# Five edits to the seams of a PE-bound fp32r network kernel: mixer output, rotation tables, lag-kernel join, re-layouts, input buffers

## The chip, the core and the metric

One program on one core of a Trainium2 chip. The metric is the device time of one execution in microseconds; the kernel before ran in 1490.31, 1491.07 and 1494.53 us, median 1491.07 us.

## The reference, cut to what matters

Two blocks of two layers on a 256 x 1024 activation, all in float32. Every norm is an rms norm over the row.

```
x += rms(even_mixer(rms(x)));   x += rms(cross_attn(rms(x), mem));  x += rms(mlp(rms(x)))    # layer 0
x += rms(band_attn(rms(x)));    x += rms(cross_attn(rms(x), mem));  x += rms(mlp(rms(x)))    # layer 1
x += diff_attn(rms(x));         x += mlp(rms(x))                                             # second block
x += s5(rms(x));                x += mlp(rms(x))

even_mixer(h): u, q, f, i, g = split(h @ w_in)
    o = gated_recurrence(q, k(f), i, log f)                 # 4 heads of 128
    return concat(pooled(u), rmsnorm(o) * out_gain * silu(g)) @ w_out
diff_attn(u):  q, k, v = split(u @ w_qkv)                   # 8 heads, two maps each
    q, k = rope(rms(q) * q_gain), rope(rms(k) * k_gain)     # cos and sin tables
    a = softmax(q0 k0) - lam * softmax(q1 k1)               # lam from four vectors
    return rms(a @ v) * subln * (1 - lam_init) @ w_o
s5(u): y = scan(u; A, B, C) + reversed scan(u; ...) + d * u # 64 groups of 16 channels, 64 states
    val, gate = split(gelu(y) @ w_glu);  return val * sigmoid(gate)
mlp(h): return relu(h @ w1)**2 @ w2                         # 1024 -> 4096 -> 1024
```

## The kernel before, in words

X lies in SBUF as two token tiles t of 128 rows by 1024. Each weight is loaded by SP in 512 KB pieces (`raw`, L42) and split into a high part `whi` (ACT, L47 or L53 with a gain) and a low part `wlo` (DVE, L49 or L58, some on POOL). Each product takes three matmuls on PE (L217 to L219 for 128x512, L224 to L226 for 128x256). X reaches the feature layout through PE transposes (`tp`, L140), a copy `hh` on ACT (L143) and a difference `hl` on DVE (L144).

`mlp` (L275) has eight chunks: chunks 0 and 1 through `ff1_a` and transposes (`fftp`, L345), the rest through `ff1_b`, each followed by the `ff2` of the chunk two before it into the accumulators `ffacc`; the last `ff2` takes two chunks and ends token tile 0 ahead of tile 1, each with `done`, that is `residual` (L178): mean square `ms` on ACT (L168), `r` on DVE and POOL (L170, L171), X on DVE (L200). Between its steps an MLP draws pieces from a generator `fill`. In the MLP of layer 1 that is `ssm_tables` for blocks 0 to 7, in the first MLP of the second block the same for blocks 8 to 15, then `ssm_prefetch`.

Per block, `ssm_tables` loads `bc`, `pk` and `gb` (SP), forms `bb`, `er` and `gr` by complex products (`cmul`: DVE, with the products `cmt` of some on POOL, L1165 and L1166), writes `gr` to DRAM (`d_g`), transposes `er` on PE (`etp`) and writes it (`d_e`), forms the lag kernels `kl` and writes them (`d_kl`, L1434). After its eight blocks it joins them in DRAM (`d_ks`, two DMAs, L1450 and L1451) and spreads them to step tables (`d_tt`, eight DMAs, L1456), all issued by POOL.

In the middle of the layer-1 MLP `reorder` writes X to DRAM and loads it back in another token order (L1791); `scales` then takes the row scale of the reordered X again, from inside chunk 5 (L383 to L389). `diff` (L639) loads its cosines, sines, gains and lambda vectors at its start, turns them into the rotation tables `ta` and `tb` (L656 to L674), then projects k, q and v; `prep` normalises and rotates a projected part (`y` on POOL L731, `z` on DVE) before it is transposed (`tq`). `ssm` (L1497) lays X out by groups (`xp`: 48 copies over DVE, ACT and POOL, L1522 to L1526), transposes (`utp`), and forms states and outputs from units `e`, `g` and `t` that SP loads from `d_e`, `d_g` and `d_tt` (L1482). In the even mixer, `vg` (L1092) takes each token tile's recurrence `o`, normalises it into `y` (L1119 to L1124) and transposes it (`otp`, L1127); `proj_a` then accumulates `pacc`.

The order on each engine is set by a planner that walks the program in the written order with priorities: `low(n)` lets instructions be taken n steps later, `now()` and `turns` say how far a projection goes before it takes up the callbacks that wait in `later`, and `manual_schedule(engines=...)` keeps the written order on the named engines. Pools whose tiles wait by tile decide when a buffer is free.

## Time and profile before

| | |
|---|---|
| profiled execution | 1488.93 us, of which span 1487.2 us |
| median of three runs | 1491.07 us |
| PE busy | 1414.7 us, 95% |
| DVE, ACT, POOL busy | 74%, 58%, 16% |
| chain that ended last | PE 73%, DVE 13%, DMA 6%, issue 4%, ACT 3% |
| mean granted TensorE clock | 0.985 of full speed |

Stages along the span, in us: even mixer 0 to 140, cross attention to 270, MLP to 470, band and cross attention to 640, MLP of layer 1 to 847, diff attention to 965, MLP to 1183, s5 to 1285, last MLP to the end. PE is the engine to look at first; what it does not do is a list of gaps, each with what ended it, and stretches at a clock of 0.50.

### The profile page before, as it was taken

Reading aid. Unit: us, or ns where it says so; the run is one execution under the profiler, and the core shown is the slowest. Engines: PE = TensorE matmul, PEld = TensorE weight load, DVE = VectorE, ACT = ScalarE, POOL = GpSimd, SP = SyncE. Lnnn points to the kernel's source line nnn. Section 1 sums busy time; section 2 is a strip of 40 time slices with the busy share of each in tenths; the row PEclk is TensorE's granted clock in tenths of the full one; section 3 lists DMA queues with packets and bytes.
Section 4 is the critical chain, followed back from the end, with each engine's and each line's share of the span. In section 5 each row is a group of like instructions: output and inputs, shape, how many; then the busy total and the mean of one; then the engine's idle time right before and its main releaser. Section 6 shows DMA issues by size and latency. Waiting matters only on the chain.

```text
span 1487.2 us, 25549 instructions
## 1 busy us (share of the span) xinstructions
PE 1414.7 (95%) x9668; PEld 1231.5 (83%) x9668; DVE 1103.8 (74%) x1965; ACT 859.4 (58%) x1480; POOL 234.4 (16%) x290
## 2 busy tenths in 40 slices
PE   8899999999999999999999789999999878999997
PEld 8897888998889798878888667888889666889895
DVE  7996658997676866569998589889995487665651
ACT  7475547565564665566656557667656463554540
POOL 1232001000010000014634210033551200000000
PEclk9999999999999999999999999999999998999999
DMA  8465535475875356366677734357779977455640
GB/s 302 143 198 170 185 125 177 157 257 193 287 256 184 119 180 200 112 207 207 220 242 265 254 124 142 100 161 241 238 236 334 346 280 262 153 187 180 210 159 29
DMA packets 121236, 298.26 MB, mean 201 GB/s; under 512 B 15129, under 2 KB 24121, under 8 KB 120473
## 3 DMA queue, kind: packets, MB, share of 16 engines
q1 hardware_dynamic: 113848, 271.40, 55.3%
q0 software_dynamic: 7264, 25.24, 4.6%
q8 instruction: 76, 1.25, 0.3%
q14 instruction: 48, 0.39, 0.1%
HBM read 270.15 MB, written 31.62 MB: 203 GB/s over the span
## 4 chain that ended last, share of the span: by engine, by line
PE 73%; DVE 13%; DMA 6%; issue 4%; ACT 3%; POOL 1%; SPq 0%; DVEq 0%; ACTq 0%; POOLq 0%
PE ffacc L217 7%; PE ffacc L219 7%; PE ffacc L218 7%; PE ffps L224 5%; PE ffps L226 5%; PE ffps L225 5%; PE pacc L219 4%; PE pacc L218 4%; PE pacc L217 4%; DVE wlo L58 3%; PE pb L225 3%; PE pb L224 3%; PE pb L226 3%; DMA raw<-in_w_ff 2%; PE ffps L219 2%
## 5 line engine op out<-in xcount | busy, mean ns | idle before, releaser
L58 DVE SCALAR_TENSOR_TENSOR wlo<-raw,gcols,whi 128x512 fp32r<-128x512 f32 (+1 forms) x456 | 356.7, 826 | 75.6 <-ACT whi L53 75.3
L53 ACT ACTIVATE whi<-raw,gcols 128x512 fp32r<-128x512 f32 (+1 forms) x456 | 317.0, 745 | 104.4 <-PE pb L226 17.3
L47 ACT ACTIVATE whi<-raw 128x1024 fp32r<-128x1024 f32 x176 | 182.8, 1055 | 155.6 <-DMA raw<-in_w_ff 59.3
L49 DVE TENSOR_TENSOR wlo<-raw,whi 128x1024 fp32r<-128x1024 f32 x172 | 210.1, 1241 | 84.1 <-ACT whi L47 80.1
L224 PE MATMUL ffps<-hh,whi 128*128 128x256 f32 x768 | 220.2, 287 | 2.7 <-ACT eo L1419 1.5
L226 PE MATMUL ffps<-hl,whi 128*128 128x256 f32 x768 | 218.2, 284 | 0.0
L225 PE MATMUL ffps<-hh,wlo 128*128 128x256 f32 x768 | 217.6, 283 | 0.0
L217 PE MATMUL ffacc<-whi,ah 128*128 128x512 f32 x512 | 204.7, 400 | 0.0
L219 PE MATMUL ffacc<-whi,al 128*128 128x512 f32 x512 | 202.2, 395 | 0.0
L218 PE MATMUL ffacc<-wlo,ah 128*128 128x512 f32 x512 | 202.1, 395 | 0.0
L224 PEld LDWEIGHTS ffps<-hh,whi 128*128 128x128 f32 x768 | 146.0, 190 | 5.3 <-ACT eo L1419 2.0
L225 PEld LDWEIGHTS ffps<-hh,wlo 128*128 128x128 f32 x768 | 145.7, 190 | 0.6
L226 PEld LDWEIGHTS ffps<-hl,whi 128*128 128x128 f32 x768 | 145.8, 190 | 0.0
L219 PEld LDWEIGHTS ffacc<-whi,al 128*128 128x128 f32 x512 | 96.4, 188 | 22.7
L217 PEld LDWEIGHTS ffacc<-whi,ah 128*128 128x128 f32 x512 | 96.5, 188 | 22.5 <-issue 1.8
L218 PEld LDWEIGHTS ffacc<-wlo,ah 128*128 128x128 f32 x512 | 96.5, 189 | 20.8
L225 PE MATMUL pb<-hh,wlo 128*128 128x256 f32 x352 | 101.2, 289 | 2.6 <-DVE wlo L58 2.6
L224 PE MATMUL pb<-hh,whi 128*128 128x256 f32 x352 | 101.2, 290 | 2.2 <-ACT whi L53 2.2
L226 PE MATMUL pb<-hl,whi 128*128 128x256 f32 x352 | 100.8, 287 | 0.0
L171 POOL TENSOR_TENSOR r<-r,mhalf 128x1 f32<-128x1 f32 x32 | 23.3, 730 | 463.9 <-DVE r L170 457.4
L303 ACT ACTIVATE relu<-ffps 128x512 f32<-128x512 f32 x64 | 43.8, 685 | 54.9 <-PE ffps L226 36.4
L225 PEld LDWEIGHTS pb<-hh,wlo 128*128 128x128 f32 x352 | 68.4, 195 | 3.4 <-DVE wlo L58 3.3
(488 smaller groups left out, 3024.9 us busy)
## 6 DMA issues: line engine op xcount, KB each, us to landing
raw<-in_w_ff SPq DMA_DIRECT2D x128, 512.0 KB, 4.6
raw<-in_ffn_w_up SPq DMA_DIRECT2D x64, 512.0 KB, 4.7
raw<-in_ffn_w_down SPq DMA_DIRECT2D x64, 512.0 KB, 4.6
raw<-in_w_mem_kv SPq DMA_DIRECT2D x32, 512.0 KB, 4.7
raw<-in_w_qkv SPq DMA_DIRECT2D x24, 512.0 KB, 4.7
raw<-in_attn_w_qkv SPq DMA_DIRECT2D x24, 512.0 KB, 5.0
raw<-in_w_in_ab SPq DMA_DIRECT2D x20, 512.0 KB, 6.5
raw<-in_w_mem_q SPq DMA_DIRECT2D x16, 512.0 KB, 4.6
```

Source lines behind the costliest of these rows:

```text
L47: nc.scalar.activation(out=hi, in_=src, func=AF.Copy)
L49: eng.tensor_tensor(out=lo, in0=src, in1=hi.bitcast(F32), op=ALU.subtract)
L53: nc.scalar.activation(out=hi[:, a], in_=src[:, a], func=AF.Copy, scale=g)
L58: nc.vector.scalar_tensor_tensor(out=lo[:, a], in0=src[:, a], scalar=g, in1=hi[:, a].bitcast(F32), op0=ALU.mult, op1=ALU.subtract)
L171: nc.gpsimd.tensor_tensor(out=r, in0=r, in1=self.mhalf[:, 0:1], op=ALU.pow)
L217: nc.tensor.matmul(o, xh, wh[:, s], start=first, stop=False)
L218: nc.tensor.matmul(o, xh, wl[:, s], start=False, stop=False)
L219: nc.tensor.matmul(o, xl, wh[:, s], start=False, stop=last)
L224: nc.tensor.matmul(out, wh, xh, start=first, stop=False)
L225: nc.tensor.matmul(out, wl, xh, start=False, stop=False)
L226: nc.tensor.matmul(out, wh, xl, start=False, stop=last)
L303: nc.scalar.activation(out=o, in_=ps if view is None else ps.rearrange("p (f c j) -> p f c j", f=2, j=8), func=AF.Relu)
```

## The change

Line numbers after the change are up to 27 higher. Five edits:

1. Even mixer: the transposes of `y` and what follows become a callback `features`, queued in `later` for both token tiles; `proj_a` takes both up with `now=(1, 2)`. The second tile's `y` has a buffer of its own.
2. Layer-1 MLP: the two `row_scale` calls move from chunk 5 to right behind chunk 3's `out_b`, with ACT's order pinned there.
3. Rotation tables and their four loads leave `diff` for a function `rotations`, called ahead of the layer-1 MLP with low priority; the lambda and sub-norm factors go behind k0 of `diff`.
4. `join` copies one block's lag kernels from `d_kl` to `d_ks` (two DMAs per block) while the next block's tables are made; `step_tables(0)` (block 7's join, eight `d_tt` DMAs) is issued inside `diff` behind k0's preparation, `step_tables(1)` in `ssm` behind the `xp` copies; POOL's order is pinned at both places; `d_tt` becomes two tensors.
5. `bc` gets 5 buffers for 3; `pk` and `gb` 4 for 2.

```diff
         def scales():
             for t in range(2):
-                if perm:
-                    self.row_scale(t)
                 q = self.small.tile([128, 1], F32, tag=f"rsq{t}", name="rsq")
...
-            parts[ch] = out_b(ps)
+            if perm and ch == 3:
+                with self.tc.manual_schedule(engines={nc.scalar.engine}):
+                    parts[ch] = out_b(ps)
+                    for t in range(2):
+                        self.row_scale(t)
+            else:
+                parts[ch] = out_b(ps)
...
         a = part(D)
-        rotations()
         for t in range(2):
             nc.vector.tensor_copy(out=rr[:, t:t + 1], in_=self.r[t])
-        k0 = prep(0, a, "k", put_k[0])
+        with self.tc.manual_schedule(engines={nc.gpsimd.engine}):
+            k0 = prep(0, a, "k", put_k[0])
+            self.step_tables(0)
         a = part(0)
         k0()
+        factors()
...
-            for h in range(4):
-                nc.tensor.transpose(tp[:, h, :], y[:, h, :], self.ident)
...
-        self.proj_a(hh, hl, w_out, 0, done, turns=HALF, share=True)
+            self.later.append(features)
+
+        self.proj_a(hh, hl, w_out, 0, done, turns=HALF, share=True, now=(1, 2))
...
+                    if g2 == 0 and k > blocks[0]:
+                        self.join(k - 1)
...
-            nc.gpsimd.dma_start(out=ks[a0:a1, :, :, 112:240], in_=kl5[a0:a1, :, 0, :, 0:128])
-            nc.gpsimd.dma_start(out=ks[a0:a1, :, :, 0:112], in_=kl5[a0:a1, :, 1, :, 32:144])
...
+    def join(self, k):
+
+        kl = self.d_kl.rearrange("a (q d i) n -> a q d i n", q=4, d=2)[k]
+        ks = self.d_ks.rearrange("(a q) i n -> a q i n", q=4)[k]
+        self.nc.gpsimd.dma_start(out=ks[:, :, 112:240], in_=kl[:, 0, :, 0:128])
+        self.nc.gpsimd.dma_start(out=ks[:, :, 0:112], in_=kl[:, 1, :, 32:144])
+
+    def step_tables(self, half):
+
+        self.join(8 * half + 7)
+        for r in range(8):
+            src = bass.AP(self.d_ks.tensor, self.d_ks.offset + half * 32 * 16 * 240 + r * 16, [[240, 16], [3840, 32], [1, 128]])
+            self.nc.gpsimd.dma_start(out=self.d_tt[half][r * 16:r * 16 + 16], in_=src)
...
-        for t in range(2):
-            x5 = X[:, t].rearrange("p (h s q e) -> p h s q e", h=2, s=4, q=8)
+        with self.tc.manual_schedule(engines={G.engine}):
+            for t in range(2):
+                x5 = X[:, t].rearrange("p (h s q e) -> p h s q e", h=2, s=4, q=8)
...
+            self.step_tables(1)
...
+        if l == 1:
+            c.rot_pool = tc.tile_pool(name="rot", bufs=1, side="right", reuse_waits="tile")
+            c.rotations(c.rot_pool.__enter__(), A["attn_q_gain_2"], A["attn_k_gain_2"], A["cos"], A["sin"])
```

DVE where the layer-1 MLP ends and `diff` begins; `ffacc_7392/7393` are the sums of token tile 0, `7394/7395` of tile 1, `qkg`, `ta`, `tb` the rotation tables, `lp`, `ls`, `nlam` lambda. Before:

```order
L187 TENSOR_TENSOR y<-ffacc_7392,gB 128x512
L187 TENSOR_TENSOR y<-ffacc_7393,gB 128x512
L170 TENSOR_SCALAR r<-ms 128x1
L58 SCALAR_TENSOR_TENSOR wlo<-raw,gcols,whi 128x512 x16
L661 TENSOR_SCALAR qkg<-qkg 128x64
L663 TENSOR_TENSOR ta<-cos,qkg 128x64
...
L673 TENSOR_TENSOR nlam<-ls 128x1
L674 TENSOR_SCALAR nlam<-nlam 128x1
L194 TENSOR_TENSOR r<-r,rsq 128x1
L200 SCALAR_TENSOR_TENSOR X<-y,r,X 128x512 x2
L187 TENSOR_TENSOR y<-ffacc_7394,gB 128x512
L187 TENSOR_TENSOR y<-ffacc_7395,gB 128x512
```

The same place now; tile 0 is `ffacc_7421/7422`, tile 1 `7423/7424`:

```order
L187 TENSOR_TENSOR y<-ffacc_7421,gB 128x512
L187 TENSOR_TENSOR y<-ffacc_7422,gB 128x512
L170 TENSOR_SCALAR r<-ms 128x1
L194 TENSOR_TENSOR r<-r,rsq 128x1
L200 SCALAR_TENSOR_TENSOR X<-y,r,X 128x512 x2
L58 SCALAR_TENSOR_TENSOR wlo<-raw,gcols,whi 128x512 x3
L170 TENSOR_SCALAR r<-ms 128x1
L58 SCALAR_TENSOR_TENSOR wlo<-raw,gcols,whi 128x512 x3
L144 TENSOR_TENSOR hl<-tp,hh 128x512 x2
L58 SCALAR_TENSOR_TENSOR wlo<-raw,gcols,whi 128x512 x4
L187 TENSOR_TENSOR y<-ffacc_7423,gB 128x512
L187 TENSOR_TENSOR y<-ffacc_7424,gB 128x512
```

X of tile 0 stood behind sixteen `wlo`, thirteen rotation instructions and the lambda factors; now it follows `r` at once, and the rotation instructions stand far up, in the MLP. On PE tile 0's eight `tp` moved from behind the last `ffacc` to 24 matmuls ahead of it, and tile 1's stand 21 `acc` matmuls behind it.

POOL between two blocks of the layer-1 MLP, where `d_kl` ends a block and `cmt` are POOL's products for the next. Before:

```order
L1434 DMA d_kl<-kl 128x144
L1408 DMA d_g<-gr 128x1024
L1165 TENSOR_TENSOR cmt<-pk,bb 128x512
L1166 TENSOR_TENSOR cmt_8773<-pk,bb 128x512
L1420 DMA d_e<-eo 128x512 x2
L1165 TENSOR_TENSOR cmt<-pk,bc 128x512
L1166 TENSOR_TENSOR cmt_8818<-pk,bc 128x512
```

Such a place now:

```order
L1451 DMA d_kl<-kl 128x144
L171 TENSOR_TENSOR r<-r,mhalf 128x1
L1470 DMA d_ks<-d_kl 64x1x128
L1471 DMA d_ks<-d_kl 64x1x112
L1435 DMA d_e<-eo 128x512
L1423 DMA d_g<-gr 128x1024
L1435 DMA d_e<-eo 128x512
L1180 TENSOR_TENSOR cmt<-pk,bb 128x512
L1181 TENSOR_TENSOR cmt_8128<-pk,bb 128x512
```

Two `d_ks` that read what the `d_kl` just above them wrote now stand between a block's end and the next `cmt`.

DVE at the start of `ssm`, where the two X updates L200 are token tiles 0 and 1. Before:

```order
L49 TENSOR_TENSOR wlo<-raw,whi 128x1024 x2
L200 SCALAR_TENSOR_TENSOR X<-ffacc_11131,rsq,X 128x512
L200 SCALAR_TENSOR_TENSOR X<-ffacc_11132,rsq,X 128x512
L170 TENSOR_SCALAR r<-ms 128x1
L1522 TENSOR_SCALAR xp<-X,r 32x16x16 x11
L1522 TENSOR_SCALAR xp<-X,r 32x8x16 x22
L1577 TENSOR_TENSOR ra<-z,tbs 128x512
```

Now:

```order
L1545 TENSOR_SCALAR xp<-X,r 32x16x16 x11
L49 TENSOR_TENSOR wlo<-raw,whi 128x1024 x2
L200 SCALAR_TENSOR_TENSOR X<-ffacc_11156,rsq,X 128x512
L200 SCALAR_TENSOR_TENSOR X<-ffacc_11157,rsq,X 128x512
L170 TENSOR_SCALAR r<-ms 128x1
L1545 TENSOR_SCALAR xp<-X,r 32x8x16 x22
L1601 TENSOR_TENSOR ra<-z,tbs 128x512
```

Tile 0's eleven `xp` copies moved ahead of tile 1's last update of X; tile 1's twenty-two stayed behind it.

## Rows read from the trace of the kernel before

**Rows 1.** The page: busy time of the engines.

```profile
PE 1414.7 (95%) x9668; PEld 1231.5 (83%) x9668; DVE 1103.8 (74%) x1965; ACT 859.4 (58%) x1480; POOL 234.4 (16%) x290
```

**Rows 2.** Waits of PE, whole span: total us, times, longest us.

```profile
PE tp L140 <- issue: 11.1, 1, 11.1
PE utp L1538 <- DVE xp L1522: 9.2, 1, 9.2
...
PE fftp L345 <- ACT relu L307: 3.1, 1, 3.1
PE otp L1127 <- DVE y L1124: 2.7, 2, 2.0
...
PE tq L742 <- DVE z L736: 2.0, 1, 2.0
```

**Rows 3.** Windows: length, busy us by engine, granted clock, DMA share, GB/s.

```profile
668.00:672.00 4.00, 4.00 (x24) 4.00 (x23) 4.00 (x6) 1.98 (x2) 2.64 (x2) 0.62 0.47 136
852.00:862.30 10.30, 3.94 (x13) 3.16 (x14) 7.51 (x29) 3.85 (x11) 0.55 (x1) 0.50 0.52 174
```

**Rows 4.** Windows over the two table-making stretches, same columns.

```profile
680.00:836.00 156.00, 150.66 (x1140) 131.43 (x1139) 133.53 (x198) 95.62 (x157) 67.71 (x78) 1.00 0.71 238
1000.00:1160.00 160.00, 160.00 (x1235) 141.82 (x1234) 135.26 (x203) 96.95 (x169) 71.08 (x82) 1.00 0.76 266
```

**Rows 5.** Timeline of PE in the even mixer: start, us, instruction, [idle before].

```profile
123.12 0.40 PE L218 MATMUL pacc<-wlo,hh 128*128 128x512 f32 x1
123.35 0.40 PE L219 MATMUL pacc<-whi,hl 128*128 128x512 f32 x1
125.78 0.63 PE L1127 MATMUL otp<-ident,y 128*128 128x128 f32 x4 [2.03 <-DVE y L1124]
```

**Rows 6.** Timeline of ACT in the layer-1 MLP.

```profile
659.70 0.64 ACT L168 ACTIVATE junk<-X 128x512 f32<-128x512 f32 x1 [6.47 <-DMA X<-d_x]
```

**Rows 7.** Timeline of DVE from the layer-1 MLP into `diff`.

```profile
837.69 0.21 DVE L170 TENSOR_SCALAR r<-ms 128x1 f32<-128x1 f32 x1 [0.85 <-ACT junk L168]
...
857.51 1.41 DVE L200 SCALAR_TENSOR_TENSOR X<-y,r,X 128x512 f32<-128x512 f32 x2
858.96 1.29 DVE L187 TENSOR_TENSOR y<-ffacc,gB 128x512 f32<-128x512 f32 x2
...
863.10 1.42 DVE L200 SCALAR_TENSOR_TENSOR X<-y,r,X 128x512 f32<-128x512 f32 x2
```

**Rows 8.** Timeline of PE at the same place.

```profile
858.36 1.94 PE L140 MATMUL tp<-ident,X 128*128 128x128 f32 x8 [11.09 <-issue]
```

**Rows 9.** Timeline of POOL at the same place.

```profile
839.38 0.77 POOL L171 TENSOR_TENSOR r<-r,mhalf 128x1 f32<-128x1 f32 x1
```

**Rows 10.** Waits of POOL, 645 to 850 us.

```profile
POOL cmt L1165 <- issue: 22.1, 7, 5.7
```

**Rows 11.** DMA issues: count, KB each, median us to landing.

```profile
d_tt<-d_ks POOLq DMA_DIRECT2D x16, 256.0 KB, 5.5
t<-d_tt SPq DMA_DIRECT2D x8, 512.0 KB, 11.3
d_kl<-kl POOLq DMA_DIRECT2D x16, 72.0 KB, 3.6
d_ks<-d_kl POOLq DMA_DIRECT2D x2, 224.0 KB, 5.1
```

**Rows 12.** Instructions that touch `d_ks`: ns min/median/max, first and last start.

```profile
L1456 POOL DMA_DIRECT2D d_tt<-d_ks x16: 630/630/654, 834.2 to 1155.8; - x16
```

**Rows 13.** DVE groups by form, 1170 to 1200 us: busy, mean ns.

```profile
L1522 DVE TENSOR_SCALAR xp<-X,r 32x128 f32<-32x128 f32 x22 | 6.2, 280 | 0.3
L1522 DVE TENSOR_SCALAR xp<-X,r 32x256 f32<-32x256 f32 x11 | 4.0, 360 | 0.1
```

**Rows 14.** Timeline of POOL at the start of `ssm`.

```profile
1186.34 3.55 POOL L1526 TENSOR_SCALAR xp<-X,r 32x128 f32<-32x128 f32 x5
```

**Rows 15.** Timeline of PE in `ssm`.

```profile
1221.28 0.64 PE L1607 MATMUL yp<-t,ut 128*32 128x128 f32 x16 [0.16 <-DMA t<-d_tt]
```

More of the change, by code (lines that the diff above doesn't have):

```diff
@@ L637, in band, with rotations @@
         self.proj_a(oh, ol, w_o, 0, done, turns=TAIL)
-    def diff(self, pool, w_qkv, gain, q_gain, k_gain, lam_vecs, subln, w_o, cos2, sin2, done):
+    def rotations(self, pool, q_gain, k_gain, cos2, sin2):
         nc = self.nc
@@ L648, in diff @@
         nc.sync.dma_start(out=gk, in_=k_gain.partition_broadcast(128))
-        sg = pool.tile([128, KT], F32, tag="sg", name="sg")
-        nc.sync.dma_start(out=sg, in_=subln)
-        lv = pool.tile([128, 4, 64], F32, tag="lv", name="lv")
-        nc.sync.dma_start(out=lv, in_=lam_vecs.partition_broadcast(128))
-        nlam = pool.tile([128, 1], F32, tag="nlam", name="nlam")
-        tabs = {}
-        def rotations():
+        self.tabs = {}
+        with self.low(600):
             for nm, g in (("k", gk), ("q", gq)):
@@ L665, in rotations, with diff, factors @@
                     nc.vector.tensor_tensor(out=tb[:, t, 32:64], in0=sn[:, t, 32:64], in1=g[:, 0:32], op=ALU.mult)
-                tabs[nm] = (ta, tb)
+                self.tabs[nm] = (ta, tb)
+    def diff(self, pool, w_qkv, gain, lam_vecs, subln, w_o, done):
+        nc = self.nc
+        tabs = self.tabs
+        sg = pool.tile([128, KT], F32, tag="sg", name="sg")
+        lv = pool.tile([128, 4, 64], F32, tag="lv", name="lv")
+        nlam = pool.tile([128, 1], F32, tag="nlam", name="nlam")
+        def factors():
+            nc.sync.dma_start(out=sg, in_=subln)
+            nc.sync.dma_start(out=lv, in_=lam_vecs.partition_broadcast(128))
             nc.vector.tensor_scalar(out=sg, in0=sg, scalar1=1.0 - LAM0, scalar2=None, op0=ALU.mult)
@@ L1120, in even @@
             r = self.rstd(ss, 4, 1.0 / 128.0)
-            y = self.sb.tile([128, 4, 128], F32, tag="y", name="y")
+            y = pool.tile([128, 4, 128], F32, tag="t2", name="y") if t else self.sb.tile([128, 4, 128], F32, tag="y", name="y")
             for h in range(4):
@@ L1155, in ssm_scratch @@
         self.d_ks = dram.tile([NG, 16, 240], F32, name="d_ks")
-        self.d_tt = dram.tile([128, NG, 128], F32, name="d_tt")
+        self.d_tt = [dram.tile([128, NG // 2, 128], F32, name=f"d_tt{i}") for i in range(2)]
     def cmul(self, pool, outr, outi, xr, xi, yr, yi, neg_i=False, tag="ct", second=None):
@@ L1446, in ssm_tables @@
                 yield
-            a0, a1 = blocks[0], blocks[-1] + 1
-            kl5 = self.d_kl.rearrange("a (q d i) n -> a q d i n", q=4, d=2)
-            ks = self.d_ks.rearrange("(a q) i n -> a q i n", q=4)
-            nc.gpsimd.dma_start(out=ks[a0:a1, :, :, 112:240], in_=kl5[a0:a1, :, 0, :, 0:128])
-            nc.gpsimd.dma_start(out=ks[a0:a1, :, :, 0:112], in_=kl5[a0:a1, :, 1, :, 32:144])
-            yield
-            n = 4 * (a1 - a0)
-            for r in range(8):
-                src = bass.AP(self.d_ks.tensor, self.d_ks.offset + 4 * a0 * 16 * 240 + r * 16, [[240, 16], [3840, n], [1, 128]])
-                nc.gpsimd.dma_start(out=self.d_tt[r * 16:r * 16 + 16, 4 * a0:4 * a1, :], in_=src)
-            yield
+            yield
+    def join(self, k):
[8 more added lines that the diff above has]
+            self.nc.gpsimd.dma_start(out=self.d_tt[half][r * 16:r * 16 + 16], in_=src)
     def ssm_prefetch(self):
@@ L1478, in load_units @@
         if kind == "t":
-            src = self.d_tt[:, 8 * i:8 * (i + n), :].rearrange("p (a g) n -> p a (g n)", g=8)
+            i4 = i % 4
+            src = self.d_tt[i // 4][:, 8 * i4:8 * (i4 + n), :].rearrange("p (a g) n -> p a (g n)", g=8)
         else:
```

43 lines of the change are left out of this document (23 added, 20 removed).

## The prediction

> **What bounds the kernel now.** I read the page's engine line first: PE is busy 1414.7 of 1487.2 us, 95% [rows 1]. The reader is to see that no other engine comes near, so only what moves PE's gaps counts, and an engine that is 74% busy, as DVE is, can still own one of them. Next come the waits of PE: one of 11.1 us before `tp`, one of 9.2 before `utp`, 3.1 before `fftp`, 2.7 in two before `otp`, 2.0 before `tq` [rows 2]. The "issue" behind the first only says that the last releaser isn't seen; DVE's timeline further down names it. Third the windows for TensorE's clock: behind the 11.1 us gap it is granted at 0.50, the lower of its levels (1.2 GHz), over 852.0 to 862.3, and behind the 3.1 us gap the mean of 668 to 672 is 0.62 [rows 3]. So a gap can cost more than its length: what PE does in such a stretch takes twice as long. Fourth the two MLPs in which tables are made: PE is busy 150.66 of 156 us in one and 160.00 of 160 in the other, DVE 133.5 and 135.3 [rows 4]; there is little to win there and something to lose.
>
> The sum goes against the profiled execution, 1488.93 us (span 1487.2 and 1.7 around it); the median of the runs is 2.1 higher, 1491.1. A measurement of this kernel can tell about 0.3%, 4.5 us, from no change.
>
> **Mixer output.** Before, 24 `pacc` matmuls, 0.23 us apart, stand between tile 0's `o` and its `otp`, 5.6 us; `otp` then waits 2.03 us for `y` [rows 5], so `y` takes 7.6 us, and tile 1's, behind 22 matmuls (5.1 us), some 5.8 (the second wait is 2.7 - 2.0 = 0.7 [rows 2]). Now both tiles' `o` come first (tile 1's eight, at the same pitch, are 1.8 us) and 36 `pacc` (8.4 us) stand ahead of both `otp`. Counted from the end of tile 0's `o`, PE arrives after 10.2 us; tile 1's `y` is there 1.8 + 5.8 = 7.6 us in if nothing is in its way, and 1.8 + 7.6 + 2.7 = 12.1 if it takes as long as tile 0's, which had a `wlo` ahead of it, and is held up by tile 0's for as long as both waits of `otp`. Between no wait and 1.9 I take 1.0: gain 1.7, between 0.5 and 2.7.
>
> **Row scale in the layer-1 MLP.** ACT stands idle 6.47 us for the reordered X to land, with all its further work (`whi`, `relu`) queued behind this row scale [rows 6]; PE's 3.1 us wait for ACT's `relu` follows from it. One chunk of this MLP is about 26 us (640 to 847 over eight), so behind chunk 3's `relu` X has long landed and ACT does not wait. Gone are 3.1 us, and of the stretch at 0.62 about (1 - 0.62) x 4 = 1.5 us, since at half speed as much again is lost as is worked. What is late next is the `raw` loads, whose buffers ACT frees. I take 4, between 2 and 4.6.
>
> **Rotation tables out of `diff`.** Tile 0's X needs one `r` (837.69), yet its update starts at 857.51, behind sixteen `wlo`, the rotation instructions and the lambda factors [rows 7]: that is the 11.1 us, since PE's `tp` starts at 858.36, right behind the first half of the update, and `ffacc` had ended at 847.3 [rows 8]. Now the update follows `r`: 837.69 + 0.21, POOL's step of 0.77, which stood behind the eight `d_tt` until 839.38 [rows 9], DVE's short product and 1.41 give about 840.3. PE takes tile 0's `tp` 24 matmuls before the end of `ffacc`, at 841.7: no wait, 1.4 us to spare. Tile 1's X took 858.96 to 864.52, 5.6 us from its `y` [rows 7]; its `ffacc` now ends at 848.2, with tile 0's `tp` (0.9) inside, so with 0.5 us behind a `wlo` X is there at 854.3, and PE, with 21 `acc` matmuls (4.9 us) in between, comes at 853.1: 1.1 us stay. The stretch at the lower clock held 3.9 us of PE's work [rows 3], which at full clock is 2.0 shorter. 11.1 + 2.0 - 1.1 = 12.0. At best nothing stays (13.1); at worst tile 1 waits behind three `wlo` more (0.83 each) and the gain is 9.5. The thirteen instructions themselves cost DVE some 1.6 us in the MLP, beside 22.5 us of DVE idle there [rows 4]: nothing. Behind k0, POOL now has ten DMA issues and a wait before k1's `y`; and the wait of `tq` for `z` [rows 2] has other `wlo` ahead of it. I put this at 0, between -2.0 (as long a wait again) and +2.0 (that wait gone).
>
> **Join block by block.** Instead of two pairs of `d_ks` there are sixteen, fourteen of them new inside the MLPs. Each waits on POOL for the `d_kl` issued just above it, 3.6 us to landing [rows 11], and the two take 1.3 us to issue, 0.65 each like a `d_tt` [rows 12]: 4.9 us, 69 us in all, beside 177 us in which POOL is idle there (156 - 67.7 and 160 - 71.1 [rows 4]). Queued behind them are POOL's `cmt` for the next block, and for these waits DVE's `er` and `gr`, ahead of `wlo`. POOL now stands 22.1 us ahead of seven such `cmt` anyway, 3.2 each [rows 10], so a `cmt` comes 4.9 - 3.2 = 1.7 us later, 24 us over fourteen. DVE's idle time covers it: 22.5 + 24.7 us, 3.4 per block [rows 4]. Not all of it lies in the right place; I take an eighth, 3 us lost. On the other side the extra `bc`, `pk` and `gb` buffers, with loads that go out earlier, can win at most PE's idle 5.3 us of the first MLP [rows 4], nothing in the second; I take 2. Together -1, between -6 (a quarter lost, nothing won) and +4.
>
> **Start of `ssm`.** PE waits 9.2 us for `xp` [rows 2]. DVE's copies are eleven of 0.360 for tile 0 and twenty-two of 0.280 for tile 1 [rows 13]; `utp` needs the first group and half of the second, 4.0 + 3.1 us. Tile 0's now run ahead of tile 1's X update. Tile 1's can't begin before its `r`, which POOL's own copies follow at 1186.34 [rows 14]; 3.1 us of copies later it is 1189.4, and with 0.4 to PE's start 1189.8, where 4.0 us of copies are gone and 1.0 is spent waiting for `r`: 3.0 us earlier. But `d_tt` for blocks 8 to 15 is written only now: POOL's copies end at 1189.9 [rows 14], two `d_ks` issues (1.3) and their landing (5.1), eight `d_tt` issues (5.0) and landing (5.5) give 1206.8, and SP's load of `t` (11.3 [rows 11]) 1218.1. PE uses it at 1221.28 now [rows 15], 1218.3 if the stage is 3.0 us earlier: no slack is left. Should both writes take what `t` takes (11.3 each), it is 1230.1, a loss of 8.8. I take 1.5, between -8.8 and +3.0; what the stage saves at its start is partly waited for again at the loads of `t` and `g`.
>
> On this term a page of the Trainium skill speaks against the change. The longest issue of a `d_tt` is 654 ns [rows 12], none of them beside DVE's `xp`. "SBUF — State Buffer", in the section "SBUF: two separate sides", says that while DVE runs an instruction in a two-port mode POOL can't write the descriptors of a DMA that it issues. DVE's copies run to about 1192.5; by the rule POOL's first issue would wait up to 2.6 us and the term would be -1.1 in place of 1.5; no row shows such a wait.
>
> **Sum.** 1.7 + 4 + 12 + 0 - 1 + 1.5 = 18.2. The profiled execution would be 1470.7, and a median on the scale of the three runs 1491.1 - 18.2 = 1473.
>
> **Rivals.** (a) POOL's joins pass through to PE. Place: between `d_kl` and the next `cmt`; price: 1.7 us on each of fourteen blocks, 24. It decides from 19.2 / 14 = 1.4 us per block, where it eats the other terms: 1491.1 - 19.2 + 24 = 1496, slower. For it: PE has no gap at all in the second MLP, so every delay there is new [rows 4]. Against: 3.4 us of DVE idle per block. 6%. (b) The late step tables: 8.8 us lost in `ssm`, with the joins at -6, leave 1.7 + 4 + 12 - 6 - 8.8 = 2.9: 1488, no change that can be told. For it: `t` has no slack. Against: it needs both landings at twice their median. 7%. (c) The 11.1 us gap turns in part into a new wait, behind POOL's pinned order or the `wlo` ahead of k0's `z`: half of the 12 stays, 1479. For it: the sixteen `wlo` are still to be made beside both updates. Against: 1.4 us to spare for tile 0. 17%. (d) The row-scale pin does nothing, because PE's 3.1 us wait comes from the `raw` loads that stand still at the same time: 1477. For it: PE waits for `relu` [rows 2], not for the row scale itself. Against: `relu` stands behind the row scale on ACT. 5%.
>
> **How the numbers follow.** The forecast has 65%, with a range of its own of 1465 to 1481 from the terms' middle bounds. Faster by over 0.3% is below 1486.6: the forecast, (c) and (d), 0.87. Same is (b), 0.07; slower is (a), 0.06. All bounds on the good side together give 1491.1 - 29.4 = 1462, which is not likely; the range is 1463 to 1486, leaving out (a), (b) and a little below.
>
> **What would show it.** In the profile after, PE's waits: `tp` "issue" gone and no window at 0.50 near 850; `fftp` gone; `utp` near 6; `otp` near 1. Windows over the table stretches with PE within 2 us of 150.66 and 160.00 per length show the joins hidden; waits of POOL at `d_ks` of 3.6 each with PE waiting for `wlo` or `er` there would show (a). A wait of `yp` for `t` above 3 us shows (b). The prediction is wrong if the stage from 640 to 865 is not at least 12 us shorter, or if the second MLP is longer by more than 3.

## The result and the profile after

The changed kernel is slower. Its median is 1508.31 us (1506.08 to 1509.71, four runs) against 1491.89 (1490.31 to 1494.53, four runs): a ratio of 1.0107, 95% interval [1.0086, 1.0127]. The forecast was 1473, with a range of 1463 to 1486. The profiled execution took 1509.71 us, its span 1507.9.

The page's engine line, which answers to [rows 1]:

```profile
PE 1432.5 (95%) x9668; PEld 1242.9 (82%) x9668; DVE 1102.8 (73%) x1965; ACT 860.6 (57%) x1480; POOL 254.6 (17%) x318
```

PE has the same share of a longer span. (In the lines below, `xN` counts the instructions of a row, and the bracket holds the idle time before it and what ended that.) It is busy 17.8 us longer for the same work, at a mean granted clock of 0.974 instead of 0.985: part of the loss is waits, part is matmuls that run slower behind them. PE's waits (line, what it waited for: us in all, times, longest), for [rows 2]:

```profile
PE ffps L224 <- ACT eo L1434: 6.5, 2, 5.5
PE utp L1562 <- DVE xp L1545: 6.2, 1, 6.2
PE fftp L345 <- ACT relu L307: 5.6, 1, 5.6
PE tq L751 <- DVE z L745: 5.1, 2, 3.4
PE tp L140 <- DVE y L834: 4.9, 3, 2.6
...
PE otp L1140 <- DVE y L1135: 0.5, 1, 0.5
```

The 11.1 us before `tp` are gone, `utp` fell from 9.2 to 6.2 and `otp` from 2.7 to 0.5. But `fftp` rose from 3.1 to 5.6, `tq` from 2.0 to 5.1, and `ffps` for `eo` and `tp` for `y` are new at this size; `eo` before:

```profile
PE ffps L224 <- ACT eo L1419: 1.5, 2, 1.0
```

Cut at PE's own landmarks (first `tp` of a stage, last `ffacc`), the stages differ as follows; the differences add up to that of the spans, 20.7 us, but for rounding. The seam is what lies between the last `ffacc` of the layer-1 MLP and tile 1's `tp` in `diff`.

| stretch of PE, us | before | after | gain forecast | gain found |
|---|---|---|---|---|
| start to the end of the even mixer | 152.9 | 151.1 | 1.7 | 1.8 |
| to the layer-1 MLP | 480.1 | 481.2 | 0 | -1.1 |
| layer-1 MLP to its first `ffacc` | 47.1 | 50.5 | 4 | -3.4 |
| first to last `ffacc` of it | 167.1 | 174.8 | part of -1 | -7.7 |
| seam, to tile 1's `tp` | 18.1 | 7.3 | 12 | 10.8 |
| `diff` | 118.4 | 135.4 | 0 | -17.0 |
| second MLP with tables | 199.8 | 199.6 | part of -1 | 0.2 |
| `ssm` | 104.1 | 108.4 | 1.5 | -4.3 |
| last MLP | 189.7 | 189.8 | 0 | -0.1 |

In other profiles the same stage in the same order came out up to 3 us apart (`diff` 135.4, 132.2 and 132.4; `ssm` 108.4 and 105.3), so smaller differences of a stage are not argued from, and the loss of `diff` is 14 to 17 us by the profile that is taken.

**Where `diff` lost 17 us.** The windows of the stage, before (length, then busy us and count of PE, PEld, DVE, ACT, POOL, the clock, DMA share, GB/s):

```profile
865.30:983.70 118.40, 113.52 (x610) 92.46 (x609) 102.94 (x231) 79.66 (x162) 12.24 (x12) 1.00 0.40 125
```

and after:

```profile
864.90:1000.30 135.40, 122.45 (x605) 97.78 (x606) 106.96 (x239) 81.75 (x167) 18.43 (x22) 0.92 0.41 133
```

PE stands idle 13.0 us for 4.9, which is 8.1, and is busy 8.9 longer for the same matmuls, at a mean clock of 0.92 instead of 1.00. DVE's timeline names the instruction behind both: k1's rotation, `z<-z,y` and `z<-z,r`. Before:

```profile
903.04 1.21 DVE L713 TENSOR_REDUCE ss<-junk 128x16 f32<-128x1024 f32 x1
904.17 1.21 DVE L734 TENSOR_TENSOR z<-z,y 128x1024 f32<-128x1024 f32 x1
...
912.99 1.29 DVE L736 TENSOR_TENSOR z<-z,r 128x512 f32<-128x512 f32 x2
```

After:

```profile
903.73 1.21 DVE L722 TENSOR_REDUCE ss<-junk 128x16 f32<-128x1024 f32 x1
...
945.69 1.22 DVE L743 TENSOR_TENSOR z<-z,y 128x1024 f32<-128x1024 f32 x1
...
947.43 1.28 DVE L745 TENSOR_TENSOR z<-z,r 128x512 f32<-128x512 f32 x2
```

The `ss` ahead of it runs at the same time in both, but `z` comes 41.5 us later, 71 rows further down in DVE's order. POOL, which now has ten DMA issues ahead of k1's `y`, is not late on the chip. Its timeline before:

```profile
899.56 2.40 POOL L731 TENSOR_TENSOR y<-kc,ta 128x1024 f32<-128x1024 f32 x1 [22.45 <-ACT kc L706]
```

and after:

```profile
882.21 5.00 POOL L1478 DMA_DIRECT2D d_tt<-d_ks  x8 [2.36 <-DMA d_ks<-d_kl]
900.27 2.90 POOL L740 TENSOR_TENSOR y<-kc,ta 128x1024 f32<-128x1024 f32 x1 [13.07 <-ACT kc L715]
```

The last `d_tt` is issued at 887.2, and `y` waits another 13 us for ACT's `kc`, until 900.27; it came at 899.56 before. So the ten issues hold up nothing on the chip, and what moved `z` is the order that the planner wrote. Why it wrote it so, perhaps because it reckoned `y` late, no run shows. PE's order is another too: 87 `acc` matmuls stand in one block instead of in pieces between the scores, which leaves less to run during the softmax; PE waits 3.4 us for `z`, then for `y`.

**Where the layer-1 MLP lost.** The clock's windows (as above) of the two gaps in it, and at the seam where [rows 3] had 0.50:

```profile
676.00:680.00 4.00, 2.28 (x11) 2.28 (x12) 4.00 (x4) 3.10 (x6) 1.72 (x2) 0.50 0.08 18
810.00:820.00 10.00, 6.64 (x36) 6.65 (x37) 2.47 (x4) 4.83 (x8) 1.67 (x3) 0.66 0.84 296
850.00:862.00 12.00, 12.00 (x57) 9.81 (x56) 10.37 (x18) 9.90 (x21) 2.31 (x1) 1.00 0.72 223
```

The slow stretch at the seam is gone; two others came. For the one at 810, ACT after:

```profile
804.83 1.99 ACT L47 ACTIVATE whi<-raw 128x1024 fp32r<-128x1024 f32 x2
811.76 1.06 ACT L47 ACTIVATE whi<-raw 128x1024 fp32r<-128x1024 f32 x1 [4.94 <-DMA raw<-in_w_ff]
812.72 1.07 ACT L1434 ACTIVATE eo<-etp 128x512 f32<-128x512 f32 x2
```

and DVE after:

```profile
799.73 1.22 DVE L49 TENSOR_TENSOR wlo<-raw,whi 128x1024 fp32r<-128x1024 f32 x1
...
805.70 4.62 DVE L49 TENSOR_TENSOR wlo<-raw,whi 128x1024 fp32r<-128x1024 f32 x4
```

Read backwards: PE waits for `eo`; ACT's `eo` stands behind a `whi` that waits 4.94 us for its weights; that load goes out when DVE's second `wlo` frees the buffer, and this `wlo` stands behind the `gr` instructions, done only at about 806.9 (805.70 plus 1.2). The experiments tell whether POOL's DMA issues or the order itself put it there.

For the gap at 676, SP's wait for X before:

```profile
SPq L42 <- DMA X<-d_x: 0.9, 1, 0.9
```

SP after, first its waits, then its issues:

```profile
SPq L1402 <- DMA X<-d_x: 5.3, 1, 5.3
SPq L1400 <- DMA X<-d_x: 2.4, 1, 2.4
```

```profile
648.41 1.29 SPq L1818 DMA_DIRECT2D X<-d_x  x2
...
654.60 2.70 SPq L42 DMA_DIRECT2D raw<-in_w_ff  x2
659.73 0.33 SPq L1400 DMA_DIRECT2D pk<-d_p  x1
665.36 0.33 SPq L1402 DMA_DIRECT2D gb<-in_ssm_g  x1
667.73 3.72 SPq L42 DMA_DIRECT2D raw<-in_w_ff  x2
```

The row-scale pin did free ACT from its wait for X [rows 6]. But SP's DMAs count their completion on eight semaphores in turn (in the trace each DMA's semaphore is that of the one eight issues before), so the loads of `pk` and `gb`, eight places behind the two reloads of X, can't be issued until X has landed: their waits end 11 and 16 us after the reloads went out. No weight load goes out between 657.3 and 667.7. ACT waits 8.1 us for `raw` instead of 6.5 for X, and PE 5.6 instead of 3.1.

### The profile page after: what moved, and what is told of

The parts are those of the page before. It is cut to its first block, busy times and chain, and to the rows that moved or that the text cites. A ratio compares the mean times of both kernels' runs of the same rounds, so it can differ in the third digit from the quotient of the medians.

```text
span 1507.9 us, 25560 instructions
## 1 busy us (share of the span) xinstructions
PE 1432.5 (95%) x9668; PEld 1242.9 (82%) x9668; DVE 1102.8 (73%) x1965; ACT 860.6 (57%) x1480; POOL 254.6 (17%) x318
## 4 chain that ended last, share of the span: by engine, by line
PE 72%; DVE 11%; DMA 6%; ACT 4%; issue 4%; POOL 2%; SPq 0%; DVEq 0%; ACTq 0%; POOLq 0%
PE ffacc L217 7%; PE ffacc L219 7%; PE ffacc L218 7%; PE ffps L224 5%; PE ffps L226 5%; PE ffps L225 5%; PE pacc L217 4%; PE pacc L219 4%; PE pacc L218 4%; PE pb L226 3%; PE pb L224 3%; PE pb L225 3%; DVE wlo L58 2%; DMA raw<-in_w_ff 2%; PE ffps L219 1%
## 5 line engine op out<-in xcount | busy, mean ns | idle before, releaser
L58 DVE SCALAR_TENSOR_TENSOR wlo<-raw,gcols,whi 128x512 fp32r<-128x512 f32 (+1 forms) x456 | 351.7, 814 | 68.8 <-ACT whi L53 68.2
L49 DVE TENSOR_TENSOR wlo<-raw,whi 128x1024 fp32r<-128x1024 f32 x172 | 213.5, 1261 | 83.3 <-ACT whi L47 76.7
L171 POOL TENSOR_TENSOR r<-r,mhalf 128x1 f32<-128x1 f32 x32 | 26.8, 836 | 470.3 <-DVE r L170 463.4
```

Of the source, the lines that this page charges most:

```text
L49: eng.tensor_tensor(out=lo, in0=src, in1=hi.bitcast(F32), op=ALU.subtract)
L58: nc.vector.scalar_tensor_tensor(out=lo[:, a], in0=src[:, a], scalar=g, in1=hi[:, a].bitcast(F32), op0=ALU.mult, op1=ALU.subtract)
L171: nc.gpsimd.tensor_tensor(out=r, in0=r, in1=self.mhalf[:, 0:1], op=ALU.pow)
```

## The experiments

Each kernel starts from the changed one unless its paragraph says otherwise, and is timed beside the kernel before; a ratio above 1 is slower than before. The medians of the kernel before lay between 1489.25 and 1492.08 us, so two paragraphs are compared by their ratios, and the times of stages are from one profile each.

**Step tables behind k1.** `step_tables(0)` stays in `diff`, pinned one preparation later.

```diff
-        with self.tc.manual_schedule(engines={nc.gpsimd.engine}):
-            k0 = prep(0, a, "k", put_k[0])
-            self.step_tables(0)
+        k0 = prep(0, a, "k", put_k[0])
...
-        k1 = prep(1, part(D + 512), "k", put_k[1])
+        a = part(D + 512)
+        with self.tc.manual_schedule(engines={nc.gpsimd.engine}):
+            k1 = prep(1, a, "k", put_k[1])
+            self.step_tables(0)
```

> The changed kernel with step_tables(0) pinned behind k1's preparation in diff, not behind k0's. Theory: the planner put DVE's z of k1 some 70 instructions late, because POOL's y of k1 stood behind ten DMA issues in its order; the rest of diff then ran one part after the other. With the tables behind k1 the z stands where it did before: the stage from tile 1's tp to the X transposes of the next MLP goes from 135.4 back to about 118.4 us, and the total from 1508 to about 1491. Rival (traffic and DVE load): the stage is longer because the d_tt writes and the wlo now share it; then it stays near 135 and the total near 1508.

Measured 1495.91 us, 1.0045 [1.0027, 1.0063], by the ratios 0.6% or 9 us below the changed kernel; `diff` took 124.4 instead of 135.4, so of the 17 us that were expected back 11 came. DVE's k1 rotation here:

```profile
903.89 1.21 DVE L743 TENSOR_TENSOR z<-z,y 128x1024 f32<-128x1024 f32 x1
...
912.71 1.29 DVE L745 TENSOR_TENSOR z<-z,r 128x512 f32<-128x512 f32 x2
```

With the same ten issues behind k1's `y` instead of ahead of it, `z` is back where it was before. Of the 6 us that remain, a `tp` that waits 3.5 us for `y` is the largest wait.

**Half 1's step tables in the MLP.** `step_tables(1)` leaves `ssm` for the end of the second MLP's generator.

```diff
+            if blocks[0] == 8:
+                self.step_tables(blocks[0] // 8)
```

> The changed kernel with step_tables(1) issued at the end of the table generator in the MLP before ssm, as before the change; the xp order stays. Theory: in ssm PE waited 2.9 us for t out of a d_tt written late, so the ssm stage (last ffacc to the X transposes of the last MLP, 108.8 us after, 104.5 before) falls to about 102, under before by the 3.0 us of the earlier xp; total about 1502. Rival: the stage is longer because PE meets val ahead of its hh and the chain on DVE is the bound; then the stage stays within 1 us of 108.8 and the total at 1508.

Measured 1503.79, 1.0094 [1.0069, 1.012]. `ssm` took 104.8, near the 104.1 of before and not the 102 I expected, and `utp` waits 9.2 us again: the early `xp` copies were tied to the pinned place of the tables, and went with it. The gain at the start of `ssm` and the late tables could not be had apart in this way.

**Former buffers.** `bc`, `pk`, `gb` with 3, 2, 2 buffers again.

```diff
-                    bc = pool.tile([128, 4, 4, 16], F32, tag="bc", name="bc", bufs=5)
+                    bc = pool.tile([128, 4, 4, 16], F32, tag="bc", name="bc", bufs=3)
...
-                    pk = pool.tile([128, 4, 34], F32, tag="pk", name="pk", bufs=4)
+                    pk = pool.tile([128, 4, 34], F32, tag="pk", name="pk", bufs=2)
...
-                    gb = pool.tile([128, 4, 16], F32, tag="gb", name="gb", bufs=4)
+                    gb = pool.tile([128, 4, 16], F32, tag="gb", name="gb", bufs=2)
```

> The changed kernel with 3, 2 and 2 buffers for bc, pk and gb. The orders of PE, ACT and POOL are the same as in the changed kernel. Theory: with more buffers SP sends more small loads ahead of the weights, and two of them wait for the reordered X to land (7.7 us in all), which holds the weight loads and so PE's 5.6 us wait at fftp; without them the layer-1 MLP (214 us from its first tp to the end of ffacc, 203 before) gets 5 to 8 us shorter and the total about 1502. Rival: buffers don't matter, the MLP is longer by the joins or the rotations: total 1508 within 2.

Measured 1509.59, 1.0136 [1.0112, 1.016]. The theory failed: `fftp` still waits 5.6 us, SP still waits for X (5.1 and 2.6 us), and first to last `ffacc` of the layer-1 MLP takes 174.9 for 174.8. The second MLP took 203.2 instead of 199.6; if that holds beyond this one profile, the buffers are worth some 3.6 us beside the joins, in the MLP where I gave them nothing.

**Joins at the end.** The two large joins again, inside `step_tables`.

```diff
-                    if g2 == 0 and k > blocks[0]:
-                        self.join(k - 1)
...
-        self.join(8 * half + 7)
...
+        self.nc.gpsimd.dma_start(out=ks[a0:a1, :, :, 112:240], in_=kl5[a0:a1, :, 0, :, 0:128])
+        self.nc.gpsimd.dma_start(out=ks[a0:a1, :, :, 0:112], in_=kl5[a0:a1, :, 1, :, 32:144])
```

> The changed kernel with all eight blocks joined by two large DMAs inside step_tables, as before the change, and no join between blocks. Theory: the joins cost PE little, since POOL waited only 10.7 and 3.8 us at them in the two MLPs; the layer-1 MLP stays within 2 us of 214. Rival (the joins' waits reach PE through cmt and er): it gets 5 us or more shorter, total 1503 or less. The diff stage may move for its own reason, the place of k1's z.

Measured 1489.36, 0.9995 [0.9978, 1.0011], by the ratios 1.1% or 17 us below the changed kernel. First to last `ffacc` takes 166.9, as before: the joins block by block cost the layer-1 MLP its 7.7 us, as the rival had it. `diff` also falls, to 127.0, though `step_tables(0)` is still pinned behind k0. Here k1's `y` starts at 892.28, with only the two `d_ks` between it and k0's, and the `d_tt` come after it:

```profile
895.12 5.00 POOL L1480 DMA_DIRECT2D d_tt<-d_ks  x8
```

Still k1's `z<-z,y` starts 13.2 us behind its `ss` (1.1 before, 42.0 in the changed kernel). So `z` is put back here too, though by less, with two issues ahead of `y` instead of ten.

**Joins two blocks late.** `join(k - 2)`, so that the `d_kl` it reads is a block older.

```diff
-                    if g2 == 0 and k > blocks[0]:
-                        self.join(k - 1)
+                    if g2 == 0 and k > blocks[0] + 1:
+                        self.join(k - 2)
...
+        self.join(8 * half + 6)
         self.join(8 * half + 7)
```

> The changed kernel with each block joined one block later (k - 2), so that its d_kl landed long ago when POOL comes to it; as many issues as in the changed kernel. Theory: the cost of the joins in the layer-1 MLP is the wait for the landing, on the chip or in the planner's order; without it the stretch from the fourth fftp's ffacc to its end falls from 174.8 to about 168 and the total from 1508 to about 1501. Rival (the fourteen more issues on POOL cost it): it stays at 174.

Measured 1512.59, 1.0154 [1.0133, 1.0175]: no better in the layer-1 MLP (175.2), worse in the second (204.7). POOL's waits for `d_kl` in the layer-1 MLP fell from 10.7 to 5.5 us and won nothing there, which speaks against the wait for the landing, the mechanism of my rival (a). DVE's second `wlo` stands behind `gr` here too, so this run does not tell the issues from the order.

**Joins late in the plan.** The joins stay block by block, but with a lower priority in the planner. DVE's order at the gap is then that of the kernel with the joins at the end:

```diff
-                        self.join(k - 1)
+                        with self.low(600):
+                            self.join(k - 1)
```

> The changed kernel with one edit: the joins inside the MLPs carry a lower priority in the planner, by 600. All sixteen DMA issues are still made block by block on POOL, but at the place in question (block 6 of the layer-1 MLP) DVE's second `wlo` stands ahead of the `gr` chain again, as in the kernel with the joins at the end; in the changed kernel it stood behind. Theory, order: the seconds lost in the layer-1 MLP come from where the planner put that `wlo` (it frees a weight buffer five instructions later, the load lands 4.8 us later, ACT's `eo` waits behind it, and PE waits 5.5 us for `eo`). Then ffacc of the layer-1 MLP ends near the 166.9 us that the kernel with the joins at the end took, not 174.8, with PE's wait for `eo` at most 2 us; the time is about 7 below the changed kernel, near 1500. Rival, the issues themselves: 1.3 us of descriptor writing on POOL per block hold up `cmt` and with it DVE; then it stays between 173 and 178, since just as many issues are made, and the time stays near 1506.

Measured 1501.54 (1493.69 to 1504.34, five runs), 1.007 [1.0039, 1.0101]; first to last `ffacc` took 167.6. DVE here, for the two rows shown above:

```profile
799.23 3.22 DVE L49 TENSOR_TENSOR wlo<-raw,whi 128x1024 fp32r<-128x1024 f32 x2
```

PE's wait for `eo` in this MLP:

```profile
PE ffps L224 <- ACT eo L1434: 0.9, 1, 0.9
```

POOL's wait at the joins in this MLP, first here, then in the changed kernel:

```profile
POOL d_ks L1471 <- DMA d_kl<-kl: 15.2, 3, 6.7
```

```profile
POOL d_ks L1470 <- DMA d_kl<-kl: 10.7, 6, 4.3
```

All the joins are still issued, POOL even waits longer for their data, and the 7 us are gone. The second `wlo` now follows the first at once. So the order theory held: the same joins cost the layer-1 MLP nothing when the `wlo` stands ahead of `gr`. By the ratios the whole gains 0.4%, some 5 us; `diff` stays at 135.8, as it should with its own cause left in.

**Joins and tables as before.** Both back at the ends of the MLPs' generators; mixer, pin, rotations and buffers as changed.

```diff
-            self.step_tables(0)
...
-                        self.join(k - 1)
...
+            if True:
+                self.step_tables(blocks[0] // 8)
             yield
...
-            self.step_tables(1)
```

> The changed kernel with both halves of join and step tables issued as before the change, at the end of each MLP's table generator, two large joins; mixer, row scale, rotations, buffers and xp order stay changed. Theory: everything that was lost came through POOL's DMA issues (the joins in the layer-1 MLP, the tables ahead of k1's y, the late d_tt in ssm); without them diff takes 118.4 us from tile 1's tp, the layer-1 MLP's second part 167 to 168, ssm 104 to 105, and what remains of the gains is 11 (end of the MLP) and 2 (mixer), less 1.5 (fftp): 1491.9 - 11 = 1480, ratio 0.992. Rival (the rotations and the earlier X make the later stages longer by themselves): diff stays at 124 or more and the total at 1487.

Measured 1487.95, 0.9988 [0.9975, 1.0001], no change that can be told. The losses in `diff` (119.9) and `ssm` (103.9) are gone, but so is the gain at the seam: 16.4. That was a miss: I had put the seam down to the rotations, which are still moved here. PE's wait, and POOL beside it:

```profile
PE tp L140 <- issue: 8.3, 1, 8.3
```

```profile
835.98 3.74 POOL L1480 DMA_DIRECT2D d_tt<-d_ks  x6
839.79 0.70 POOL L171 TENSOR_TENSOR r<-r,mhalf 128x1 f32<-128x1 f32 x1
```

With the tables on POOL at that place, POOL's step for tile 0's `r` stands behind the `d_tt`, as in [rows 9]. On the chip that `r` is done at 840.5, yet DVE takes tile 0's X 15 us later, again behind sixteen `wlo`:

```profile
855.69 1.42 DVE L200 SCALAR_TENSOR_TENSOR X<-y,r,X 128x512 f32<-128x512 f32 x2
```

**Only the first step tables moved.** The kernel before, with one edit: the joins and `d_tt` of blocks 0 to 7 are issued at the start of the next MLP's generator. The rotations stay in `diff`.

```diff
             last = None
+            if blocks[0]:
+                self.step_tables(0, 8)
...
+            if blocks[0]:
+                self.step_tables(8, 16)
             yield
...
-            for r in range(8):
...
-                nc.gpsimd.dma_start(out=self.d_tt[r * 16:r * 16 + 16, 4 * a0:4 * a1, :], in_=src)
```

> The kernel before with one thing changed: the two d_ks and eight d_tt DMAs of blocks 0 to 7 are issued at the start of the next MLP's table generator, not at the end of the layer-1 MLP's. The rotations stay in diff. Theory (the place of the step tables on POOL, not the rotations, made tile 0's X late): the planner takes X of tile 0 up early, and from the end of ffacc to tile 1's tp it takes 9 to 11 us, not 18.1 (the rotations still wait for their loads ahead of tile 1's X); diff stays at 118, total 1483, ratio 0.995. Rival (the prediction's own: the rotations and lambda factors hold X): it stays at 17 to 18 us and the total at 1491.

Measured 1482.84, 0.9948 [0.9932, 0.9964]; the seam took 9.4 us instead of 18.1. Its DVE, which answers to [rows 7], and PE's wait, to [rows 8]:

```profile
838.86 1.41 DVE L200 SCALAR_TENSOR_TENSOR X<-y,r,X 128x512 f32<-128x512 f32 x2
```

```profile
PE tp L140 <- issue: 3.9, 1, 3.9
```

Tile 0's X update comes at 838.86 instead of 857.51 although the rotations are still there. They, and some `wlo`, now stand ahead of tile 1's update, where PE waits 3.9. The issues did not go as far as written: the planner took them up early, and the eight `d_tt` stand on POOL between 851.3 and 895.8 us, from the seam into `diff`.

**X by 32 rows.** The reload of X in eight DMAs of 32 rows instead of two.

```diff
-        c.nc.sync.dma_start(out=c.X[:, t], in_=token_rows(c.d_x, t))
+        for a in range(4):
+            src = bass.AP(c.d_x.tensor, c.d_x.offset + (t * 4 + a) * D, [[8 * D, 32], [1, D]])
+            c.nc.sync.dma_start(out=c.X[a * 32:a * 32 + 32, t], in_=src)
```

> The changed kernel with the reordered X loaded by eight DMAs of 32 rows, in place of two of 128 rows whose outer dimension is 4. Theory: PE's 5.6 us wait at fftp comes from SP, whose loads pk and gb wait 7.7 us for X to land, since every eighth SP DMA shares a completion count with one before it, and the weights queue behind them; X lands 16 us after its issue because each of its DMAs runs on few engines. With eight it lands within 6 us, the wait at fftp is gone and from the first tp of the MLP to the fourth fftp it takes 30 us, not 34.1. Total about 1503. Rival (the weights are late for another reason, their buffers): the wait stays above 3 us.

Measured 1503.15, 1.0088 [1.0062, 1.0114]. SP, and the landing of these DMAs:

```profile
648.62 3.58 SPq L1820 DMA_DIRECT2D X<-d_x  x8
...
653.93 1.54 SPq L42 DMA_DIRECT2D raw<-in_w_ff  x2
```

```profile
X<-d_x SPq DMA_DIRECT2D x8, 128.0 KB, 4.2
```

Each of the eight lands in a median of 4.2 us, the last of them 7.5 us after the first went out; SP's waits for X are down to 0.2 us at most, and the 5.6 us before `fftp` are gone: from tile 1's `tp` to the first `ffacc` PE takes 31.1 instead of 39.3. Of these 8.2 us 5.0 are given back between first and last `ffacc` (179.8 for 174.8), with 9.6 us of waits for `eo`. That this MLP can't end before its tables are made would explain it; no run shows that by itself.

**The same with joins and tables as before.**

```diff
+            if True:
+                self.step_tables(blocks[0] // 8)
...
+            c.nc.sync.dma_start(out=c.X[a * 32:a * 32 + 32, t], in_=src)
```

> tables_as_before and x_by_32_rows together. Theory: 1480 less 5, about 1475, ratio 0.988. Rival: no better than tables_as_before.

Measured 1485.27, 0.9966 [0.9952, 0.998]: 2.7 us below the kernel without the eight DMAs, and above the 1475 expected, which took over the 1480 that had missed. First to last `ffacc` takes 171.4 instead of 165.5.

**Tables in the next MLP.** Large joins; blocks 0 to 7 at the start of the next MLP's generator, 8 to 15 at its end; the rest as changed.

```diff
             last = None
+            if blocks[0]:
+                self.step_tables(0)
...
+            if blocks[0] == 8:
+                self.step_tables(blocks[0] // 8)
             yield
```

> The changed kernel with two large joins, the step tables of blocks 0 to 7 at the start of the next MLP's generator and those of 8 to 15 at its end. Theory: nothing of POOL's DMA work stands near diff or ssm, so the gain at the end of the layer-1 MLP (18.1 to about 7) comes without the loss in diff (118 to 120) and in ssm (104): 1490.7 - 11 - 1.5 + 1.5 = 1480, ratio 0.993. Rival: the ten DMAs at the start of the next MLP hold POOL's products there, and that MLP takes 203 us or more in place of 199.6; total 1484.

Measured 1483.62, 0.9942 [0.9928, 0.9957], for an expected 1480: seam 8.7, `diff` 118.9, second MLP 199.4. Of the places tried for the tables it is the one that costs no stage anything. It is not the place that was written: on POOL the `d_tt` again lie from the seam into `diff`, five ahead of k1's `y` (895.11) and three behind it:

```profile
872.61 1.89 POOL L1482 DMA_DIRECT2D d_tt<-d_ks  x3
...
897.43 1.89 POOL L1482 DMA_DIRECT2D d_tt<-d_ks  x3
```

Here `z` follows `ss` at once (1.1 us), with five issues ahead of `y`. With the joins at the end two were enough to put it back, so their number does not decide. Those two kernels, the changed one and that with the joins at the end, have POOL's order pinned behind k0 and this one does not; no run has the same place without the pin. The kernel before with the first step tables moved and nothing else came to the same ratio, 0.9948, so mixer, rotations, buffers and row scale together add nothing to it that can be told.

**The same without the row-scale pin.**

```diff
-            if perm and ch == 3:
-                with self.tc.manual_schedule(engines={nc.scalar.engine}):
...
+                if perm:
+                    self.row_scale(t)
```

> tables_in_next_mlp with the row scale back in chunk 5, not pinned behind chunk 3. Theory: the pin only moves the wait for X from ACT (and 3.1 us at PE) to SP (5.6 us at PE); without it the first tp of the MLP to the fourth fftp takes 32.6 us, not 34, and the total is 0 to 2 us lower than with it. Rival: the pin saves 3 us or more, so the total is that much higher without it.

Measured 1480.7, 0.9927 [0.9915, 0.9939]. PE is at its first `ffacc` 3.8 us sooner (32.9 + 3.3 against 34.7 + 5.3), and keeps 1.9 of it to the last one (169.4 against 167.5). The intervals of the two totals overlap; by the stage, edit 2 costs time where I had it gain 4.

**The same with X by 32 rows, with and without the pin.**

```diff
+            c.nc.sync.dma_start(out=c.X[a * 32:a * 32 + 32, t], in_=src)
```

> tables_in_next_mlp with X reloaded by eight DMAs of 32 rows. Theory: the 5.6 us wait at fftp goes, but the MLP is bound by the chain that makes its tables, so of it some 2 to 3 us stay, as between the two runs before (1487.95 and 1485.27): 1477, ratio 0.991. Rival: all 5.6 stay, 1474.

> The best version so far (two large joins, step tables in the next MLPs, X reloaded by 32 rows) without edit 2's pin of the row scale behind chunk 3. Theory, the pin only costs: 2 to 3 us less than the 1479.2 of the best version, near 1477. Rival, table-bound: with X landing early nobody waits for the row scale in either place, and the MLP ends when its tables do; then it is 1479 within 2 us.

Measured 1479.18, 0.9922 [0.991, 0.9935] with the pin and 1477.75, 0.9925 [0.991, 0.994] without: the same, and both faster than the kernel before and the changed one. With X quick, PE reaches its fourth `fftp` at the same point with and without the pin (27.8 and 27.9 us behind tile 1's `tp`), and neither ACT nor SP waits for X by more than 0.2 us. Of the kernels that were run this is the one to keep: mixer edit, rotations ahead, buffers, large joins, tables written into the next MLP, X by 32 rows. X by 32 rows with the first step tables moved and nothing else was not run; it may do as well.

## Why the prediction was wrong

**The failed step** is "Behind k0, POOL now has ten DMA issues and a wait before k1's `y` [...] I put this at 0", with bounds of -2.0 and +2.0. It asked whether POOL would be late, and it was not. What the tables behind k0 changed was the order, in which DVE's `z` went 71 rows down. `diff` lost 17.0 us, nearly the whole forecast gain of 18.2; with the tables behind k1 11 of them came back, with the tables out of this place all but 0.5 to 1.5. By the prediction's own sign, too, it was wrong: from the start of the layer-1 MLP to tile 1's `tp` the kernel was to be 12 us shorter and is 0.3 longer (3.4 + 7.7 - 10.8). I had the order of DVE at the seam, of POOL between blocks and of DVE in `ssm` in hand, and didn't look at DVE's order between the pinned instructions and their consumers.

**Joins and buffers**, put at -1 within -6 to +4, came to -7.7 in one MLP and +0.2 in the other, below the bounds. Rival (a) named the place and its mechanism fell: with the joins late in the plan POOL waited longer for the landings (15.2 us) and made all the issues, and the stretch took 167.6. Again the order did it.

**Row scale**, put at +4, is -3.4. That ACT no longer waits for X was right. "What is late next is the `raw` loads" had the answer, and I gave it no price: SP's queue stands still for X too. Rival (d) named those loads and expected no gain; it was a loss.

**The seam** was sized well, 10.8 against 12.0, with 2.4 us of waiting left instead of 1.1. The reason was wrong: I had put DVE's order, with X behind sixteen `wlo`, down to the rotations. The runs give it to edit 4, the step tables on POOL ahead of `r`. With the rotations moved and the tables kept the seam is 16.4; with the tables moved and the rotations kept it is 9.4. Both edits touch that place, which made them look like one cause; how the tables led the planner to that order was not tested.

**`ssm`** kept its first half: `utp` waits 6.2, as forecast. POOL after, and PE's later waits, which answer to [rows 15]:

```profile
1205.98 0.70 POOL L1470 DMA_DIRECT2D d_ks<-d_kl  x1
1206.69 0.64 POOL L1471 DMA_DIRECT2D d_ks<-d_kl  x1
1213.17 5.00 POOL L1478 DMA_DIRECT2D d_tt<-d_ks  x8 [5.84 <-issue]
```

```profile
1242.40 1.08 PE L1631 MATMUL yp<-t,ut 128*32 128x128 f32 x16 [2.91 <-DMA t<-d_tt]
...
1251.66 0.80 PE L217 MATMUL val<-whi,hh 128*128 128x512 f32 x1 [3.76 <-ACT hh L1667]
```

The wait for `t` is 2.9 instead of 0.2, and `val` waits 3.8 for ACT. In sum PE's idle time hardly changed (104.1 - 81.9 = 22.2 before, 108.4 - 87.2 = 21.2 after); the loss is 5.3 us more busy time, at a mean clock of 0.86 for 0.90: gaps in other places, slower work behind them. Rival (b) had the place and half the price, though its own sign, a wait for `t` above 3 us, is just not reached. The term had the landing of `d_tt` too short: 5.5 us was taken, a median [rows 11], and the last of the eight took 10.4, with the DMA engines at a share of 1.0. It had taken 11.6 in the kernel before. The two `d_ks` issues, which took 0.70 and 0.64 us, lie beside DVE's copies:

```profile
1202.47 6.94 DVE L1545 TENSOR_SCALAR xp<-X,r 32x128 f32<-32x128 f32 x22 [0.67 <-POOL r L171]
```

The rule of the Trainium skill that was weighed there ("SBUF — State Buffer", "SBUF: two separate sides"), by which POOL's first issue would have waited up to 2.6 us, does not show in the length of the issues. The two landed 5.6 and 6.0 us after they were issued, against 2.8 and 2.5 for the pair in `diff`; with the DMA share at 1.0 there these rows can't tell a late descriptor from busy DMA engines, and whether the copies run in a two-port mode no run shows.

**The mixer** came to 1.8 for 1.7, and `otp` waits 0.5 for 2.7; 1.1 of it was gone before the layer-1 MLP. Both are within what a stage varies, and no run took this edit alone, so the agreement may be luck.

What stays open: why 6 us of `diff` remain when the tables stand behind k1. The trace shows a `tp` 3.5 us early for its `y` and PE in another order; no run took that alone away. Open as well is how the planner came from POOL's order to DVE's, and what the pin alone did.

## What to carry to other kernels

Where a planner writes the order, an instruction that is moved to an idle engine's queue, or pinned there, is not free because the engine is idle: instructions of other engines may be ordered anew, far away. Compare the order of every engine that consumes what stands behind it, up to the end of the stage, not only where the edit is. When two edits move the same instruction, find out by runs with one each which of them did it, and before taking a wait away from one engine, ask which queue waits for the same landing.
